# Ordering one program by PSUM bank: finer dependencies, and PSUM slots kept back by fences instead of by rule

## The chip, the cores and the metric

The kernel runs on one core of a Trainium2 chip. A core has five engines with queues of their own: TensorE (PE, matmuls; its weight loads are shown as PEld), VectorE (DVE), ScalarE (ACT), GpSimd (POOL) and SyncE (SP, which here issues the DMAs). PE writes its results to PSUM, 128 partitions of eight banks of 512 fp32 numbers; ACT and DVE read them there. The metric is the device time of one execution in microseconds, as the median of several runs; lower is better.

## What is computed

One inference step of a hybrid diffusion backbone of two layers, for 512 latent tokens and 128 context tokens that share all weights. The widths are D = 1024 and 2816 in the feed-forward part, all in fp32. Cut to what matters:

```python
def trunk_layer(x, cvec, l, P, pos, ctx):
    mod = jax.nn.silu(cvec) @ P['ada_w'][l] + P['ada_b'][l]
    sh1, sc1, g1, sh2, sc2, g2 = jnp.split(mod, 6, axis=-1)
    mix, ctx_out = token_mixer(x * (1.0 + sc1) + sh1, l, P, pos, ctx)
    x = layer_norm(ALPHA * x + g1 * mix, P['ln_g'][l, 0], P['ln_b'][l, 0])
    ff = conv_ffn(x * (1.0 + sc2) + sh2, l, P)
    x = layer_norm(ALPHA * x + g2 * ff, P['ln_g'][l, 1], P['ln_b'][l, 1])
    return x, ctx_out
```

token_mixer projects its input to three parallel mixers: A is retention in both directions with a fixed decay per head, B is gated linear attention in both directions with a decay that depends on the data, C is differential attention (two softmax maps per head). Each gives 512 channels, goes through a branch matrix, is weighted by sigmoid gates (also projections) and summed; an output projection follows. conv_ffn projects up to 2 x 2816, applies a depthwise convolution of width 3 and GELU to one half, multiplies the halves and projects down. The outputs are both token groups, and the context's keys, values and final states.

## The kernel before

All 640 tokens are handled together, channels on the 128 partitions and tokens along the free axis (512 latent, then 128 context). An activation of 1024 channels is eight tiles of 128 x 640. A fp32 product is made of three fast matmuls: each operand is split into a high part (hi, hh, ...) and a rest (lo, hl, ...), and hi*hi, hi*lo and lo*hi are added up in PSUM. Weights come block by block (128 x 1024) from HBM through three staging slots (w), are split by ACT (whi) and by DVE or POOL (wlo), and a block waits for a free slot of whi and wlo.

**How the order is found.** The functions of the kernel (mix_b, mix_a, mix_c, branch, the norms, the feed-forward part) don't emit instructions. Each call of mm, act, tt, ts and so on adds an operation to a Program (Program.add): the engines that may run it, an assumed cost, and the tiles and regions that it reads and writes. Program.add derives from these which earlier operations it depends on. When all are recorded, Program.order (L261) plays the whole program through on a model of the engines, greedily: whenever an engine is free it takes, among the operations whose inputs are ready and for which all new tiles can be given a slot, the one that was recorded first (with small exceptions, such as ACT's function tables). An operation may start before earlier ones as long as it lies within 120 us of PE work of the first unfinished matmul (40 us for loads). Program.issue then emits the instructions in the order of their modelled starts, so each engine's queue on the chip is in that order; waits are put in for true dependencies. The model's times do not reach the chip, only the order does.

**Slots.** Tiles live in pools (Pool_): `r`, 59 rows of 128 x 640 in SBUF, the weights' three pools, two small ones, and two PSUM pools of two slots each, a slot being 128 x 1024, two banks. `pp` (called through slot) takes most projections, the values pvv, the branch products and the mixers' accumulators po; `pm` (called through mslot) takes mixer B's pk, the decays pz, the scores psd, psl and psp of its levels, the states pst, mixer A's and C's scores, the norms' statistics (pm, pv, pn, pca, ...), and every other tile of the output, up and down projections (pfb, odd pout and pdn). A slot is given when the first operation on a tile is placed, and comes free when the last is done.

`reserve` is a rule of a pool: while no more than that many slots are free, only the tiles that come next in program order may take one (slots, within order). The rows have 7, `pp` has RES[0] = 0 and `pm` has RES[1] = 1, so with two slots the last free one of `pm` goes to the next tile in program order only.

**Dependencies.** For a tile in SBUF, Program.add compares regions (partitions and columns). For a PSUM tile it takes every access for an access of the whole tile (L238).

**Tiles and names around the change.** A projection (project, gemm) fills columns 256 to 896 of its slot in two halves, HALF: first tokens 256 to 640 in columns 512 to 896 (384 columns, second bank), then tokens 0 to 256 in columns 256 to 512 (first bank), for each half k = 0 to 7 and three matmuls per k. Its evictions mostly read both halves; rope has one that reads the context part alone (columns 768 to 896). v_proj fills blocks of tokens, in mixer B's first pass one bank for each token block. At the start the inputs hh/hl are made k by k, both halves of a k (to_h); at the layers' border and ahead of the feed-forward part they come from norm_h, one half after the other. mix_b makes two passes (t = 0, 1) over two heads each: decays (zr with pz), scores of the same position (psd), seven levels m = 1 to 64 (psl and copies into st; psp for the context), then m = 128 and 256, and at the end po, which all chunks add to. All is ordered as described; no line sets an order by hand.

Of the kernel before, what the change touches and what calls it, by code (L numbers as in the profile page):

```python
# [131 lines left out]
DEPTH = 2  # L132
SAME = 130
GAP = 2
RES = (0, 1)


class Tile_:
# [79 lines left out]
class Program:  # L218
# [3 lines left out]
    def add(self, engs, fn, outs, ins, cost, func=None, load=False, late=0, port=()):  # L222
        op = Op()
        op.idx, op.engs, op.fn, op.cost = len(self.ops), engs, fn, cost
        op.users, op.ready, op.func, op.load, op.eng = [], 0.0, func, load, None
        op.queues, op.port = set(), port
        op.key = (op.idx + late, op.idx)
        op.coord = self.pe
        if engs[0] == "PE":
            self.pe += cost["PE"]  # L230
        deps, tiles = set(), []
        for views, write in ((ins, False), (outs, True)):
            for v in views:
                if not isinstance(v, V):
                    continue
                t, (p0, p1, c0, c1) = v.tile, v.reg
                if t.pool is not None and t.pool.psum:
                    p0, p1, c0, c1 = 0, 128, 0, 1  # L238
                if t not in tiles:
                    tiles.append(t)  # L240
                keep = []
                for a in t.acc:
                    o, w, (q0, q1, d0, d1) = a
                    hit = p0 < q1 and q0 < p1 and c0 < d1 and d0 < c1
                    if hit and (w or write) and o is not op:
                        deps.add(o)
                    if not (write and p0 <= q0 and q1 <= p1 and c0 <= d0 and d1 <= c1 and o is not op):
                        keep.append(a)
                t.acc = keep
                t.acc.append((op, write, (p0, p1, c0, c1)))  # L250
        for t in tiles:
            if not t.left and t.pool is not None:
                t.pool.want.append((op.idx, t))
            t.left += 1
        op.deps, op.tiles, op.wait = sorted(deps, key=lambda o: o.idx), tiles, len(deps)
        for d in op.deps:
            d.users.append(op)
        self.ops.append(op)
        return op

    def order(self, ahead, ahead_load):  # L261
        import heapq
        engs = ("PE", "ACT", "DVE", "POOL", "SP")
        free = {e: 0.0 for e in engs}
        now, later = {e: [] for e in engs}, {e: [] for e in engs}
        held, done = [], []
# [16 lines left out]
        def slots(op, t0):  # L283

            used = {}
            for t in op.tiles:
                if t.slot is None and t.pool is not None:
                    p = t.pool
                    u = used.get(p, 0)
                    used[p] = u + 1  # L290
                    if len(p.free) <= u:
                        p.blocked.append(op)
                        return None
                    if p.inorder or len(p.free) <= p.reserve:
                        while p.want[p.ptr][1].slot is not None:
                            p.ptr += 1
                        i, rank = p.ptr, 0
                        lim = 1 if p.inorder else len(p.free)
                        while rank < lim and p.want[i][1] is not t:
                            rank += p.want[i][1].slot is None  # L300
                            i += 1
                        if rank >= lim:
                            p.blocked.append(op)
                            return None
                    t0 = max(t0, heapq.nsmallest(u + 1, p.free)[u][0])
            return t0
# [4 lines left out]
        while len(done) < len(self.ops):  # L311
            best = None
            for e in engs:
                f, n, q = free[e], now[e], later[e]
                while q and (q[0][0] <= f or q[0][2].eng):
                    r, i, op = heapq.heappop(q)
# [3 lines left out]
                while n or q:  # L320
                    if n:
                        i, op = heapq.heappop(n)
                        if op.eng:
                            continue
                        t = slots(op, f)
                        if t is not None and e in op.port:
                            t = max(t, port)
                        if t is None:
                            op.queues.discard(e)
                            continue  # L330
                        if t > f:
                            heapq.heappush(q, (t, i, op))
                            continue
                        if e == "POOL" and len(op.engs) > 1 and max(free["DVE"], op.ready) + op.cost["DVE"] <= t + op.cost[e]:
                            waiting.append((i, op))
                            continue
                        if e == "ACT" and op.func in TABLES and not table & TABLES[op.func] and passed < 6 and len(skipped) < 6 \
                                and op.key[0] >= op.idx:
                            skipped.append((i, op))
                            continue  # L340
                        cand = (t, i, op)
                        break
                    if skipped:
                        break
                    r, i, op = heapq.heappop(q)
                    if op.eng:
                        continue
                    t = slots(op, r)
                    if t is not None and e in op.port:
                        t = max(t, port)  # L350
# [8 lines left out]
                if cand is None and skipped:  # L359
                    i, op = skipped.pop(0)  # L360
# [8 lines left out]
                    else:  # L369
                        heapq.heappush(later[e], cand)  # L370
            if best is None:
                raise RuntimeError(f"stuck after {len(done)} of {len(self.ops)} operations: " + "; ".join(
                    f"{p.name}: {len(p.free)} free" for p in {o.tiles[0].pool for o in self.ops} if p))
            (t0, i, op), e = best
            c = op.cost[e]
            if e == "ACT" and op.func in TABLES:
# [38 lines left out]
            if e == "PE":  # L415
# [3 lines left out]
                while held:  # L419
                    o = held[0][2]  # L420
# [34 lines left out]
def hybrid_kernel(ctx, tc, io):  # L455
# [8 lines left out]
    def pool(name, n, space=sb, **kw):  # L464
        def make(t):
            return space.tile(t.shape, t.dt, tag=f"{name}{t.slot}", name=t.name)

        return Pool_(name, n, make, psum=space is psum, **kw)
# [3 lines left out]
    p_small, p_tiny = pool("sm", 2), pool("ti", 24)  # L472
    p_p, p_m = pool("pp", 2, psum, reserve=RES[0]), pool("pm", 2, psum, reserve=RES[1])

# [1173 lines left out]
```

## Time and profile before

| | us |
|---|---|
| median of 3 runs | 2575.58 (2574.66 to 2575.99) |
| the profiled execution | 2572.64 |
| its span, first to last instruction | 2570.9 |
| TensorE's mean granted clock | 0.981 of full speed |

The span in 40 slices, each digit the busy share in tenths; PEclk is the granted clock in tenths:

```profile
PE   7999999999998999999989899999999999999997
DVE  6688786576688765656868877644553574334446
ACT  3586754454225322213447766544442352132224
PEclk9999999999998999999989989999999999999998
```

A row of these profiles names a line, an engine, an operation, out<-in by the tiles' names, shapes and a count. Since every matmul is recorded by one helper (L504, L513 for pairs of 64 rows, L518 for transposes), the tile's name tells the stage. "[4.73 <-DVE qq]" behind a row says that the engine stood idle for 4.73 us before it, and what released it. Matmuls are pipelined: one lasts longer than the distance to the next, so the rate is read from the starts. The first layer takes about the first half: mixers to 730 us, output projection and norm to 838, feed-forward part to some 1290; the second layer repeats it.

### The profile page before, as it was taken

The numbers are of one execution on the slowest core, as the hardware profiler recorded it, in microseconds if no ns is written. First come the engines' busy times: TensorE is split into PE (matmuls) and PEld (weight loads), VectorE is DVE, ScalarE is ACT, GpSimd is POOL, SyncE is SP. The second block draws the span as 40 slices with busy tenths as digits, with TensorE's granted clock in tenths as the row PEclk, the third lists the DMA queues.
The fourth block names the chain that finished last, engine by engine and source line by source line (L and its number), as shares of the span: only waits on it lengthen the run. The fifth ranks groups of instructions, "written<-read, shape, count | busy, mean of one in ns | idle before, by whom it ended". The sixth has DMA issues, their size and how long they took to land.

```text
span 2570.9 us, 41226 instructions
## 1 busy us (share of the span) xinstructions
PE 2469.6 (96%) x16730; PEld 2349.8 (91%) x16730; DVE 1633.3 (64%) x2897; ACT 1126.3 (44%) x1822; POOL 515.1 (20%) x381
## 2 busy tenths in 40 slices
PE   7999999999998999999989899999999999999997
PEld 4888889999997999999978788999999989999996
DVE  6688786576688765656868877644553574334446
ACT  3586754454225322213447766544442352132224
POOL 0542120121334100101446501111111140000000
PEclk9999999999998999999989989999999999999998
DMA  7122222322442333333521221212113322222223
GB/s 278 49 93 85 89 72 93 104 88 99 156 156 99 123 108 120 108 116 130 163 98 53 68 89 60 62 52 75 52 66 115 112 77 82 75 74 74 74 76 105
DMA packets 92062, 248.76 MB, mean 97 GB/s; under 512 B 10336, under 2 KB 16864, under 8 KB 91744
## 3 DMA queue, kind: packets, MB, share of 16 engines
q1 hardware_dynamic: 91872, 246.13, 28.9%
q8 instruction: 131, 2.15, 0.3%
q14 instruction: 59, 0.48, 0.1%
HBM read 238.75 MB, written 7.34 MB: 96 GB/s over the span
## 4 chain that ended last, share of the span: by engine, by line
PE 85%; DVE 8%; ACT 4%; DMA 1%; issue 1%; POOL 1%; SPq 0%; ACTq 0%; DVEq 0%; POOLq 0%
PE pmm L504 13%; PE pfb L504 12%; PE pfa L504 11%; PE pdn L504 11%; PE pbr L504 7%; PE pvv L504 6%; PE pout L504 4%; PE pck L504 2%; PE pcq L504 2%; PE pag L504 2%; PE psc L513 2%; PE ptc L504 1%; PE psl L513 1%; PE po L504 1%; DVE hl L551 1%
## 5 line engine op out<-in xcount | busy, mean ns | idle before, releaser
L525 ACT ACTIVATE whi<-w 128x1024 fp32r<-128x1024 f32 (+2 forms) x330 | 342.9, 1040 | 864.0 <-PE pdn L504 221.5
L537 DVE TENSOR_TENSOR wlo<-w,whi 128x1024 fp32r<-128x1024 f32 (+2 forms) x276 | 344.0, 1247 | 356.9 <-ACT whi L525 350.7
L537 POOL TENSOR_TENSOR wlo<-w,whi 128x1024 fp32r<-128x1024 f32 (+1 forms) x54 | 130.2, 2412 | 806.6 <-ACT whi L525 664.7
L504 PE MATMUL pmm<-hl,whi 128*128 128x384 f32 (+1 forms) x768 | 239.3, 312 | 0.0
L504 PE MATMUL pmm<-hh,whi 128*128 128x384 f32 (+1 forms) x768 | 238.9, 311 | 0.0
L504 PE MATMUL pmm<-hh,wlo 128*128 128x384 f32 (+1 forms) x768 | 238.8, 311 | 0.0
L504 PE MATMUL pfa<-hl,whi 128*128 128x384 f32 (+1 forms) x704 | 221.4, 315 | 7.2 <-DVE hl L551 6.8
L504 PE MATMUL pfa<-hh,whi 128*128 128x384 f32 (+1 forms) x704 | 219.5, 313 | 5.4 <-ACT hh L525 5.3
L504 PE MATMUL pfb<-hh,wlo 128*128 128x256 f32 (+1 forms) x704 | 220.1, 313 | 3.9 <-DVE wlo L537 3.9
L504 PE MATMUL pdn<-fh,whi 128*128 128x384 f32 (+1 forms) x704 | 217.6, 310 | 2.7 <-DVE xa L551 2.7
L504 PE MATMUL pfb<-hh,whi 128*128 128x256 f32 (+1 forms) x704 | 220.1, 313 | 0.0
L504 PE MATMUL pfb<-hl,whi 128*128 128x256 f32 (+1 forms) x704 | 219.9, 312 | 0.0
L504 PE MATMUL pfa<-hh,wlo 128*128 128x384 f32 (+1 forms) x704 | 219.5, 312 | 0.0
L504 PE MATMUL pdn<-fh,wlo 128*128 128x384 f32 (+1 forms) x704 | 218.0, 310 | 0.0
L504 PE MATMUL pdn<-fl,whi 128*128 128x384 f32 (+1 forms) x704 | 217.5, 309 | 0.0
L504 PEld LDWEIGHTS pmm<-hh,whi 128*128 128x128 f32 x768 | 144.5, 188 | 1.2 <-issue 1.1
L504 PEld LDWEIGHTS pmm<-hh,wlo 128*128 128x128 f32 x768 | 144.5, 188 | 0.9 <-issue 0.6
L504 PEld LDWEIGHTS pmm<-hl,whi 128*128 128x128 f32 x768 | 144.4, 188 | 0.9 <-issue 0.5
L504 PEld LDWEIGHTS pfa<-hl,whi 128*128 128x128 f32 x704 | 133.8, 190 | 10.5 <-DVE hl L551 10.4
L504 PE MATMUL pvv<-whi,hh 128*128 128x256 f32 (+1 forms) x480 | 138.1, 288 | 4.9 <-ACT hh L525 3.9
L504 PEld LDWEIGHTS pfa<-hh,whi 128*128 128x128 f32 x704 | 133.5, 190 | 7.4 <-ACT hh L525 7.3
L504 PE MATMUL pvv<-wlo,hh 128*128 128x256 f32 (+1 forms) x480 | 137.5, 287 | 2.7 <-DVE wlo L537 2.7
(388 smaller groups left out, 6829.2 us busy)
## 6 DMA issues: line engine op xcount, KB each, us to landing
w<-W SPq DMA_DIRECT2D x276, 512.0 KB, 3.5
wada<-adaT SPq DMA_DIRECT2D x160, 256.0 KB, 3.9
w<-W SPq DMA_DIRECT2D x48, 448.0 KB, 3.2
wada<-adaW SPq DMA_DIRECT2D x32, 256.0 KB, 5.2
x<-xT SPq DMA_DIRECT2D x8, 320.0 KB, 6.1
dist<-rc SPq DMA_DIRECT2D x8, 320.0 KB, 3.4
xa<-xT SPq DMA_DIRECT2D x8, 320.0 KB, 6.7
xsave<-xa SPq DMA_DIRECT2D x8, 320.0 KB, 6.1
```

The lines of the kernel that those rows point to most:

```text
L504: prog.add(("PE",), lambda e: nc.tensor.matmul(real(out), real(lhsT), real(rhs), start=start, stop=stop), [out], [lhsT, rhs], {"PE": c})
L513: nc.tensor.matmul(real(o), real(w), real(r), start=start, stop=stop)
L525: prog.add(("ACT",), lambda e: nc.scalar.activation(out=real(out), in_=real(in_), func=func, **{k: real(x) for k, x in kw.items()}), [out] ...
L537: prog.add(eng, lambda e: ENG[e].tensor_tensor(out=real(out), in0=real(a), in1=real(b), op=op), [out], [a, b], vcost(out.n), late=late, po ...
L551: prog.add(eng, lambda e: ENG[e].scalar_tensor_tensor(out=real(out), in0=real(a), scalar=real(s), in1=real(b), op0=op0, op1=op1), [out], [ ...
```

## The change

Three things change; no operation is added to or taken from the program that is ordered.

- In Program.add the region of an access to a PSUM tile becomes the range of 512-column banks that it touches, on all partitions, instead of the whole tile.
- RES becomes (0, 0): no slot of `pm` is kept back by rule.
- Without a reserve the order can get stuck (all slots held by tiles whose last operations need another slot). order becomes a loop around the former function, now place. If place ends with operations left over, the loop takes the first operation that has no engine, waits for no input and needs a new slot, and adds a fence for the pools concerned: as long as that operation is not placed, all operations behind it in program order must leave one slot of the pool free (two at most). Then all is reset and placed again, up to 60 times.

```diff
-RES = (0, 1)
+RES = (0, 0)
...
                 if t.pool is not None and t.pool.psum:
-                    p0, p1, c0, c1 = 0, 128, 0, 1
+                    p0, p1, c0, c1 = 0, 128, c0 // 512, -(-min(c1, 1024) // 512)
...
     def order(self, ahead, ahead_load):
+
+
+        fences, tiles = {}, {t: t.left for o in self.ops for t in o.tiles}
+        pools = {t.pool: list(t.pool.free) for t in tiles if t.pool is not None}
+        for _ in range(60):
+            done = self.place(ahead, ahead_load, fences)
+            if len(done) == len(self.ops):
+                return done
+            for f in self.ops:
+                new = [p for p in {t.pool for t in f.tiles if t.slot is None and t.pool is not None}]
+                if not f.eng and not f.wait and new and any(fences.get((p, f), 0) < 2 for p in new):
+                    break
+            else:
+                break
+            for p in new:
+                fences[p, f] = fences.get((p, f), 0) + 1
+            for o in self.ops:
+                o.eng, o.ready, o.wait, o.queues = None, 0.0, len(o.deps), set()
+            for t, n in tiles.items():
+                t.slot, t.left, t.end = None, n, 0.0
+            for p, free in pools.items():
+                p.free, p.blocked, p.ptr = list(free), [], 0
+        raise RuntimeError(f"stuck after {len(done)} of {len(self.ops)} operations")
+
+    def place(self, ahead, ahead_load, fences):
...
-                    if len(p.free) <= u:
+                    if len(p.free) <= u + sum(n for (q, f), n in fences.items() if q is p and not f.eng and op.idx > f.idx):
                         p.blocked.append(op)
                         return None
...
             if best is None:
-                raise RuntimeError(f"stuck after {len(done)} of {len(self.ops)} operations: " + "; ".join(
-                    f"{p.name}: {len(p.free)} free" for p in {o.tiles[0].pool for o in self.ops} if p))
+                break
```

## The prediction

> **What bounds the kernel now.** I read the page first: the busy line, then the chain that ended last.
>
> ```profile
> span 2570.9 us, 41226 instructions
> PE 2469.6 (96%) x16730; PEld 2349.8 (91%) x16730; DVE 1633.3 (64%) x2897; ACT 1126.3 (44%) x1822; POOL 515.1 (20%) x381
> PE 85%; DVE 8%; ACT 4%; DMA 1%; issue 1%; POOL 1%; SPq 0%; ACTq 0%; DVEq 0%; POOLq 0%
> ```
>
> TensorE (PE) is busy for 2469.6 of 2570.9 us, and 85% of the chain is PE work. The change reorders instructions and removes none, so all that it can win or lose is PE's idle time, 2570.9 - 2469.6 = 101.3 us, and time in which PE runs at a lower granted clock. Where these lie is told by busy time in 65 us stretches. Columns: stretch, its length, busy us (and instructions) of PE, its weight loads, DVE, ACT, POOL; granted clock; DMA share; GB/s.
>
> ```profile
> 0.00:65.00 65.00, 49.81 (x248) 28.18 (x249) 39.60 (x154) 25.34 (x53) 4.21 (x10) 0.95 0.74 278
> 130.00:195.00 65.00, 59.50 (x457) 53.20 (x456) 52.75 (x75) 51.18 (x100) 26.63 (x26) 1.00 0.27 92
> 195.00:260.00 65.00, 58.67 (x401) 52.63 (x401) 54.58 (x87) 44.45 (x87) 19.04 (x17) 0.92 0.28 92
> 780.00:845.00 65.00, 52.31 (x287) 47.95 (x286) 56.22 (x112) 34.24 (x58) 35.10 (x28) 0.84 0.25 81
> 1365.00:1430.00 65.00, 59.92 (x488) 53.21 (x486) 50.88 (x62) 43.32 (x85) 41.39 (x39) 0.97 0.17 56
> 1430.00:1495.00 65.00, 51.91 (x393) 45.74 (x392) 56.47 (x86) 47.58 (x94) 32.94 (x31) 0.87 0.20 65
> 2015.00:2080.00 65.00, 62.20 (x396) 60.55 (x394) 47.19 (x94) 29.69 (x44) 14.09 (x8) 0.95 0.38 122
> 2145.00:2210.00 65.00, 65.00 (x443) 65.00 (x442) 27.91 (x40) 18.10 (x21) 0.00 (x0) 1.00 0.23 73
> ```
>
> The reader should see a stretch without any idle time (2145, the feed-forward part: nothing to win) beside the start (15.2 us idle), the two passes of mixer B (130 to 260 and 1365 to 1495) and the step from the output projection to the feed-forward part (780). Now who PE waited for; columns: total us, times, longest.
>
> ```profile
> PE pq L504 <- ACT hh L525: 7.5, 5, 3.5
> PE pfa L504 <- DVE hl L551: 6.8, 6, 2.5
> PE pm L504 <- DVE acc L537: 5.2, 2, 4.1
> PE psl L513 <- DVE qq L580: 4.7, 1, 4.7
> PE po L504 <- ACT qa L525: 3.1, 1, 3.1
> PE psl L513 <- DVE st L572: 2.6, 2, 1.3
> ```
>
> The first four are waits for data, the last two for a PSUM slot still being read. Slots alone are a small part of the idle time.
>
> **Part 1: dependencies by bank (Program.add).** It removes the order between accesses of one PSUM tile that lie in different 512-column banks. Where does that free PE? A projection fills columns 512 to 896 first (the 384-column half) and then 256 to 512: by whole tiles the second half may not begin before the first is complete, by banks it may. At the start of the kernel the inputs hh/hl arrive one k at a time:
>
> ```profile
> 45.72 0.45 PE L504 MATMUL pq<-hh,whi 128*128 128x384 f32 x1 [0.60 <-ACT hh L525]
> 47.77 0.44 PE L504 MATMUL pq<-hh,whi 128*128 128x384 f32 x1 [0.58 <-ACT hh L525]
> 49.90 0.45 PE L504 MATMUL pq<-hh,whi 128*128 128x384 f32 x1 [0.53 <-ACT hh L525]
> 50.84 0.28 PE L504 MATMUL pq<-hh,whi 128*128 128x256 f32 x1
> 53.67 0.34 PE L504 MATMUL pk<-hl,whi 128*128 128x384 f32 x1
> 54.02 0.28 PE L504 MATMUL pk<-hh,whi 128*128 128x256 f32 x1
> 56.86 0.30 PE L504 MATMUL pvv<-whi,hh 128*128 128x288 f32 x1
> 57.00 0.29 PE L504 MATMUL pvv<-whi,hl 128*128 128x288 f32 x1
> ```
>
> A k arrives each 2.1 us; from 45.72 to 49.90 PE runs for each k the three wide matmuls of pq and of pk and then waits. All narrow ones come after the last wide one: pq's 24 from 50.84 to 53.67 (118 ns each), pk's 24 from 54.02 to 56.86 (118 ns each). By banks those of k = 0 to 6, 2 x 7 x 3 = 42 with 42 x 0.118 = 5.0 us, can run in the gaps: to_h writes both halves of a k before the next k. Wide ones cost 0.175 us (pk's two from 53.67 to 54.02), so six are 1.05 us of each 2.1 us, and six narrow ones 0.7 us: they fit. I take 4.5 us of the 5.0, since a mixture of two tiles never packs wholly. What hides the rest today is nothing: after 50.84 PE is busy without a gap, so the saving moves all that follows. Late next would be the weights of pvv, whose slots pq and pk free earlier by the same amount. Bounds: 0 (weights late) and 6.3 (with the nine matmuls of pvv's second token block, which lie in its other bank: 9 x 0.14 us from 56.86 to 57.00).
>
> At the border of the layers PE waits in the same way:
>
> ```profile
> 1310.33 0.29 PE L504 MATMUL pvv<-wlo,hh 128*128 128x288 f32 x1
> 1312.97 0.39 PE L504 MATMUL pq<-hh,whi 128*128 128x256 f32 x1 [2.35 <-ACT hh L525]
> ```
>
> But there half 0 of every k is made before half 1 (norm_h goes half by half), so the halves are not each other's filler. Only pvv's nine of the second token block can fill such a wait: 1 us. In the other tiles the evictions read both banks (P0:P0+T), so they stay where they are; rope's 128-column copy of the context part reads the first-filled bank alone and may go some 3 us (24 narrow matmuls) earlier, but it waits for its turn on ACT rather than for PE, so I count 0, from -1 to +3. No instruction or DMA is added, and SP's loads move only with the matmuls that free their slots.
>
> **Part 2: no slot of pool pm kept back (RES 1 to 0), with fences.** Before, the last free of the two pm slots went only to the next tile in program order. Here is what that shapes in mixer B of the second layer:
>
> ```profile
> 1347.41 0.45 PE L504 MATMUL pz<-zr,wa 128*128 128x384 f32 x2
> 1349.67 0.56 PE L504 MATMUL pz<-zr,wa 128*128 128x384 f32 x2 [0.52 <-DVE la L545]
> 1375.50 1.16 PE L513 MATMUL psl<-eq,ek 64*128 64x128 f32 x16 [1.30 <-DVE st L572]
> 1388.80 0.53 PE L504 MATMUL pz<-zr,wa 128*128 128x384 f32 x2
> 1452.01 0.28 PE L504 MATMUL paq<-hh,wlo 128*128 128x256 f32 x1
> 1477.68 0.77 PE L513 MATMUL psl<-qq,kk 128*128 128x256 f32 x2 [4.73 <-DVE qq L580]
> 1482.02 0.80 PE L513 MATMUL psl<-qq,kk 128*128 128x256 f32 x2 [1.18 <-ACT p L525]
> 1487.28 0.27 ACT L525 ACTIVATE qa<-paq 128x128 f32<-128x128 f32 x1
> 1487.61 1.65 PE L504 MATMUL po<-st,v 128*128 128x128 f32 x6 [3.05 <-ACT qa L525]
> ```
>
> The decay matmuls pz of t = 0 run at 1347 and 1349. Those of t = 1 read the same zr and wa, so they could run then, but start at 1388.80, 39 us later, when both slots are free at once. From them hangs t = 1's chain of levels, at whose end PE stands still: 4.73 + 1.18 us, then 3.05 us for a slot of the other pool, pp, which the change does not touch. Earlier decays let that chain end earlier. The value is not shown by any row, so it has two ends. The best end is all that two passes lose: in 130 to 260, 5.50 + 6.33 us idle and 0.08 x 65 = 5.2 us of clock; in 1365 to 1495, 5.08 + 13.09 us idle and (0.03 + 0.13) x 65 = 10.4 us: 45.6 us. The worst end is a loss of 18 us (rival 2). I take 6 us, the two waits of the chain's end in this row set (5.9), and nothing for the first layer, because DVE there is already busy for 52.75 and 54.58 of 65 us.
>
> The clock column bears on this: 0.87 in 1430 to 1495 costs 8.5 us beside the idle time itself. [...]
>
> **Sum.** 4.5 + 1 + 6 = 11.5 us: the span goes from 2570.9 to 2559.4. The profiled execution took 2572.64 us, 1.74 more than its span, and the median of the runs, 2575.58, lies 2.94 above that. So 2575.6 - 11.5 = 2564 us as a median.
>
> **Rivals.**
> 1. **The gain is swallowed (2573).** For it: 780 to 845 and the ends of the layers wait for data (hh, hl, acc), and a new greedy order may lose there what it wins elsewhere; the step at 780 has 12.7 us of idle time where the same step of the second layer (2015 to 2080) has 2.8, so an order alone can move 10 us. Against: the start's 4.5 us have no wait behind them that stays. About 2 to 3 us remain.
> 2. **Hoarded slots (2588, slower).** A tile far ahead takes the last pm slot and its readers do not get their turn; then t's chain has one slot, and each level waits until the level before has been read out. Price: the 1.30 us at 1375.50, where pk held the other slot. Seven levels, two t, two layers are 28; the half that has little other PE work beside it, 14 x 1.30 = 18 us; less 5.5 for part 1 it is +12.5. It decides once more than four levels are hit uncovered (4 x 1.30 = 5.2 against part 1's 5.5). For it: paq's last matmul starts at 1452.01, and its slot is held until 1487.28, so slots are held for 35 us in this kernel. Against: a fence keeps a slot back, though only where the order got stuck altogether.
> 3. **The starvation goes (2546).** t = 1's chain overlaps t = 0's wholly, in both layers: of the 45.6 us some 24 come back, with part 1's 5.5 together 29.5. Against: DVE's 52 to 56 busy us of 65 leave it little room.
> 4. **It does not do what it says** (waits on the chip remain by tile): PE would then wait for each early reader of the first bank. That is inside rival 1 up to three waits of the size of 1.30 us, and beyond that it is like rival 2.
>
> **How the numbers follow.** Forecast 2564, its own range 2557 to 2570: 0.43. Rival 1: 0.20. Rival 2, with 4's worse half: 0.25. Rival 3: 0.12. A difference under 0.2%, about 5 us, is no more than a measurement can tell from no change. Faster 0.43 + 0.12 = 0.55, same 0.20, slower 0.25. The range reaches from rival 3's middle to nearly rival 2's price: 2546 to 2586, which leaves out about half of rival 3 and something less than half of rival 2.
>
> **What would show it.** Part 1: narrow pq and pk matmuls between the wide ones before 50 us, and the first pvv after them about 5 us before 56.86. Part 2: the second pair of pz well before 1388.80 (less the shift), and a PE idle time under 10 us where 1430 to 1495 has 13.1. Rival 2: more and longer waits psl <- st than the 2.6 us above, in mixer B. The feed-forward stretches should stay at 65.00 of 65. It is wrong if idle time grows in a stretch that I count as unchanged, above all 780 to 845 and the two ends of layers.

## The result, and the profile after

The changed kernel takes 2558.41 us as a median (2556.14 to 2559.82) against 2575.5 beside it: ratio 0.9933, 95% interval 0.9916 to 0.9950, 17 us faster. The page and its busy line:

```profile
span 2554.4 us, 41254 instructions
PE 2462.3 (96%) x16730; PEld 2344.1 (92%) x16730; DVE 1635.9 (64%) x2895; ACT 1128.1 (44%) x1822; POOL 520.0 (20%) x385
```

As many matmuls as before, so the work is the same; of the 16.5 us of span 9.2 were idle time (2554.4 - 2462.3 = 92.1 against 101.3) and the rest is busy time (2462.3 against 2469.6), at a mean granted clock of 0.986 against 0.981. The same stretches as in the prediction, now of the changed kernel:

```profile
0.00:65.00 65.00, 49.84 (x246) 29.11 (x247) 37.48 (x150) 25.13 (x53) 4.27 (x10) 0.96 0.73 274
130.00:195.00 65.00, 63.14 (x499) 56.61 (x497) 55.04 (x70) 50.05 (x97) 37.64 (x36) 1.00 0.28 92
195.00:260.00 65.00, 60.76 (x410) 54.10 (x410) 55.84 (x96) 47.44 (x90) 12.89 (x10) 0.95 0.30 98
780.00:845.00 65.00, 52.70 (x306) 49.48 (x306) 59.02 (x112) 35.55 (x59) 35.99 (x28) 0.89 0.28 94
1365.00:1430.00 65.00, 63.68 (x511) 57.19 (x512) 52.48 (x64) 50.56 (x93) 37.20 (x39) 1.00 0.24 80
1430.00:1495.00 65.00, 53.83 (x414) 47.47 (x413) 57.17 (x103) 46.34 (x94) 24.65 (x25) 0.89 0.21 68
2145.00:2210.00 65.00, 65.00 (x444) 65.00 (x443) 25.59 (x39) 15.49 (x17) 0.00 (x0) 1.00 0.24 79
```

The start does as much as before (49.84 busy us, 246 instructions), mixer B of both layers does more, the feed-forward part is full as it was. And the waits of PE:

```profile
PE po L528 <- DVE qa L561: 8.7, 1, 8.7
PE pfa L528 <- DVE hl L575: 7.4, 6, 2.6
PE pck L528 <- ACT qkp L549: 2.9, 8, 0.4
PE pcq L528 <- ACT qkp L549: 2.9, 8, 0.4
PE psl L537 <- DVE st L596: 1.5, 2, 1.3
PE pvv L528 <- ACT z L549: 1.5, 4, 0.4
```

Three rows are of a new kind: pck and pcq waiting for ACT's qkp, and pvv for z. They are short and regular, and those for qkp come from rope's early copies, which the prediction had counted as 0. The first row has grown: po waited 3.05 us for qa before.

Since the operations are the same and only their order differs (and for some the engine that runs them), I compare where the kernels stand at fixed points of the program. The first line has the times before; below it is each kernel's lead or lag there (minus: earlier), read from the timeline as the start of the first matmul of that tile in that layer (for pdn and pq a fixed one of them).

```
                      start      B1       A,C1     step    border   B2      A2      C2     span
                      psl   paq   pag   pcq  pout  pdn    pq     pag   pcq   pout
before                97.4 169.1 240.6 347.4 731.8 1108.7 1313.0 1514.3 1622.7 2007.1  2570.9
changed               -0.6  +0.3  -5.4  -8.4  -2.3  -5.8   -7.1  -16.2  -20.8  -15.4   2554.4
e1_banks_only         -4.2  +0.7  +2.5  +4.7  +9.8  +5.0   +4.0   -1.1   -1.3   +3.1   2572.9
e2_slots_only         +0.7  +0.8  +1.6  -0.1  +0.1  -2.9   -3.1  -12.4  -14.3  -14.4   2557.2
e3_readers_whole      -0.4  -2.5  -7.7 -11.1  -9.6 -13.2  -16.1  -26.5  -31.2  -30.8   2538.6
e4_rope_whole         +0.8  +1.7  -4.0  -7.5  -6.7 -10.9  -13.6  -21.3  -26.0  -25.2   2545.1
e6_start_wide_first   -2.3  -4.2  -9.2 -12.6 -11.1 -15.0  -17.7  -29.3  -34.0  -33.5   2535.7
e7_start_after_ada    -4.0  -6.0 -11.7 -15.0 -13.4 -16.5  -16.2  -28.4  -33.1  -32.6   2537.8
e8_late_decays        -2.8  -2.7  +3.9  +2.4  +2.3  -2.0   -3.6   -9.9  -13.2  -12.1   2558.0
e10_rope_by_bank      -2.9  -4.9  -9.9 -12.9  -7.0 -10.4  -12.0  -23.2  -27.7  -22.2   2547.6
```

Each row is one execution, so small leads mean little. In the changed kernel and e4_rope_whole PE's rows name the same tiles in the same order to far beyond the first paq (for 2261 matmuls), and yet the two stand 1.4 us apart there; whole executions of the kernel before lie between 2570.67 and 2578.40 us.

The line "changed" tells the story. Nothing is won at the start (paq +0.3). Mixer B of the first layer wins some 6 us; mixer C and the branches give 6 back between pcq and pout (some of pcq's lead is work moved ahead, from then on 3 to 4 us are lost); the step to the feed-forward part wins 3.5; mixer B of the second layer wins 9; its mixer C gives back 5 by the same count. The step's 3.5 belong to neither part alone: every other kernel in the table wins 3.0 to 4.8 there, the banks alone and the slots alone too. Whether the kernel before loses them in each execution is not shown.

### The profile page after: what moved, and what is told of

It reads as the page before. It is cut to its first block, busy times and chain, and to the rows that moved or that the text cites. A ratio compares the mean times of both kernels' runs of the same rounds, so it can differ in the third digit from the quotient of the medians.

```text
span 2554.4 us, 41254 instructions
## 1 busy us (share of the span) xinstructions
PE 2462.3 (96%) x16730; PEld 2344.1 (92%) x16730; DVE 1635.9 (64%) x2895; ACT 1128.1 (44%) x1822; POOL 520.0 (20%) x385
## 5 line engine op out<-in xcount | busy, mean ns | idle before, releaser
L561 DVE TENSOR_TENSOR wlo<-w,whi 128x1024 fp32r<-128x1024 f32 (+1 forms) x278 | 345.0, 1242 | 363.5 <-ACT whi L549 356.8
L528 PE MATMUL pfb<-hl,whi 128*128 128x384 f32 (+1 forms) x704 | 219.6, 312 | 0.0
L528 PE MATMUL pfb<-hh,whi 128*128 128x384 f32 (+1 forms) x704 | 218.8, 311 | 0.0
```

Source lines behind the costliest of these rows:

```text
L528: prog.add(("PE",), lambda e: nc.tensor.matmul(real(out), real(lhsT), real(rhs), start=start, stop=stop), [out], [lhsT, rhs], {"PE": c})
L561: prog.add(eng, lambda e: ENG[e].tensor_tensor(out=real(out), in0=real(a), in1=real(b), op=op), [out], [a, b], vcost(out.n), late=late, po ...
```

## The experiments

### The two parts alone

```diff
 e1_banks_only
-RES = (0, 0)
+RES = (0, 1)
 e2_slots_only
-                    p0, p1, c0, c1 = 0, 128, c0 // 512, -(-min(c1, 1024) // 512)
+                    p0, p1, c0, c1 = 0, 128, 0, 1
```

> Only the dependencies by bank; pool pm keeps its last slot for the next tile in program order again. Theory (mixer B's gain of some 17 us in its two layers comes from the freed slots, and the banks bring about nothing at the start and a loss of some 3 us in each mixer C, where ACT's early copies qkp stand between the matmuls of one projection): 2575 to 2582 us, no gain in mixer B, and 16 waits of PE for ACT qkp of about 0.37 us. Rival (the banks make the gain): 2556 to 2564 us, with the earlier mixer B of the changed kernel.

> Only the freed slots with fences; PSUM dependencies by whole tile as before. Theory: mixer B's gain without the losses of the banks, 2550 to 2556 us, no waits of PE for ACT qkp, and t = 1's decays pz some 10 us or more earlier in each layer than before. Rival (the slots alone do nothing, or hoarding makes it slower): 2572 us or more.

The banks alone gave 2574.87 us, ratio 1.0002 (0.9992 to 1.0011): no change. The slots alone gave 2559.33, ratio 0.9934 (0.9917 to 0.9950): as much as the whole change. The slots bring the gain, though 3 us less than the theory's range; the banks bring nothing on balance. The table shows that the second is a balance and not a zero: with the banks alone the kernel loses 5 us from pcq to pout in the first layer and 4 in the second, and wins 5 at the step and, against the theory, 5 in mixer B of the second layer. The slots' gain lies in the second layer (pq to pag, 9 us) and at the step, not in the first layer's mixer B, where the slots alone do nothing (pag +1.6). There the 5.4 us of the changed kernel need both parts.

In the second layer the slots alone do what the prediction said of them: the waits of 4.73, 1.18 and 3.05 us at the end of t = 1's chain are gone, and the idle time from 1430 to 1495 falls from 13.09 to 6.05 us. The row of e2_slots_only:

```profile
1430.00:1495.00 65.00, 58.95 (x439) 52.52 (x437) 53.89 (x82) 41.79 (x87) 31.96 (x30) 0.89 0.16 52
```

But early decays alone don't explain it. In the first layer the decays of t = 1 start at 119.82 us instead of 142.29 in e2, 22 us earlier, and mixer B wins nothing; in the second they start at 1380.59 instead of 1388.80, only 5 us closer to t = 0's, and it wins 9.

### What the banks cost

One of the new waits, on PE's timeline of the changed kernel, and then the row of ACT that belongs to it:

```profile
454.79 0.34 PE L528 MATMUL pcq<-hh,wlo 128*128 128x384 f32 x1
454.96 0.28 PE L528 MATMUL pcq<-hh,whi 128*128 128x256 f32 x1
...
456.38 0.28 PE L528 MATMUL pcq<-hh,whi 128*128 128x256 f32 x1
456.50 0.27 PE L528 MATMUL pcq<-hl,whi 128*128 128x256 f32 x1
457.15 0.38 PE L528 MATMUL pcq<-hh,wlo 128*128 128x256 f32 x1 [0.37 <-ACT qkp L549]
```

```profile
456.82 0.28 ACT L549 ACTIVATE qkp<-pcq 128x128 f32<-128x128 f32 x1 [2.77 <-PE pcq L528]
```

ACT's copy qkp reads columns 768 to 896, the bank that the wide half had filled before the narrow matmuls (256 columns) began. The last wide one has ended at 455.13. Yet ACT, idle for 2.77 us, starts only at 456.82, just after the 14th narrow one has ended (456.50 + 0.27 = 456.77), and the 15th then waits for ACT; the other nine follow later, from 458.93. So the waits in the program treat the tile as one here: the reader waits for the matmuls that stand before it in the order, whatever their bank, and those that stand behind it wait for the reader. All 18 early copies of this run (16 qkp, 2 ka) start 0.03 to 0.05 us after the end of the matmul before them, and PE's next one starts 0.05 or 0.06 us after the copy's end. An order that takes the two banks for independent puts the reader between the matmuls, and PE pays. PE's step from 456.50 to 457.15 is 0.65 us instead of 0.12: 0.53 us for one copy. The 18 such steps of the changed kernel (16 for qkp, 2 for ka) are 0.64 to 0.73 us long.

```diff
 e3_readers_whole
-                    p0, p1, c0, c1 = 0, 128, c0 // 512, -(-min(c1, 1024) // 512)
+                    p0, p1, c0, c1 = (0, 128, c0 // 512, -(-min(c1, 1024) // 512)) if engs[0] == "PE" else (0, 128, 0, 2)
 e4_rope_whole
-        act(prompt, ps[:, P0 + TL:P0 + T])
+        act(prompt, ps[:, P0 + TL:P0 + T], also=(ps,))
```

(`also` adds its tiles to what the operation reads for the order; the instruction is the same.)

> As the changed kernel, but by banks only between accesses of TensorE; ACT's and DVE's accesses to a PSUM tile count for the whole tile. Theory (the chip's waits go by whole tile, so each reader that the order puts between the matmuls of its tile costs PE about 0.37 us, some 23 of them, 8 to 9 us): 2548 to 2553 us, and no waits of PE for qkp, ka or z. Rival (these waits cost nothing in the end, or another order loses as much elsewhere): 2556 to 2565 us.

> As the changed kernel, but rope's copy of the context part (qkp, qa, ka) counts for the whole tile. Theory: 16 + 2 waits of 0.37 us go, 6.7 us, so 2550 to 2554 us, and mixer C no longer gives back 3 us in each layer. Rival (the 3 us in each mixer C come from something else): mixer C gives back 3 us as before, 2556 to 2561 us.

e3_readers_whole gave 2542.83 us, ratio 0.9876 (0.9862 to 0.9891), and e4_rope_whole 2546.86, 0.9892 (0.9875 to 0.9908). Both are faster than the changed kernel by more than expected: 0.0057 x 2575 = 14.7 us and 10.6 us, each good to some 5 us by the intervals. In both, qkp no longer holds PE up, and mixer C gives nearly nothing back (pcq to pout 1.5 and 0.8 us where it was 6.1). In size both theories were short, because I had counted PE's idle time alone, 0.37 us where the step loses 0.53. The idle time of the weight loads is nearer to the loss:

```profile
PEld pcq L528 <- ACT qkp L549: 4.6, 8, 0.6
PEld pck L528 <- ACT qkp L549: 4.6, 8, 0.6
PEld pvv L528 <- ACT z L549: 2.4, 4, 0.6
PEld pak L528 <- ACT ka L549: 1.1, 2, 0.6
```

These four rows of the changed kernel add up to 12.7 us, beside the 14.7 of e3; qkp and ka alone are 10.3, near the 10.6 of e4. Against the slots alone, e3_readers_whole (banks between matmuls only) is faster by 0.0058, some 15 us: that is what the banks bring once no reader stands between the matmuls, and what the readers take back in the changed kernel. By the table 6 of the 15 arise in the first layer's mixer B (paq to pag); why is not shown. On the fastest base found (e6, below) I put the cost back by itself:

```diff
 e10_rope_by_bank (against e6_start_wide_first)
-                    p0, p1, c0, c1 = (0, 128, c0 // 512, -(-min(c1, 1024) // 512)) if engs[0] == "PE" else (0, 128, 0, 2)
+                    p0, p1, c0, c1 = (0, 128, c0 // 512, -(-min(c1, 1024) // 512)) if engs[0] == "PE" or self.bank else (0, 128, 0, 2)
...
+        prog.bank = True
         act(prompt, ps[:, P0 + TL:P0 + T])
+        prog.bank = False
```

> As e6_start_wide_first, but rope's copy of the context part alone counts by bank again. Theory (each such copy cuts a projection in two for PE; the idle time of PE is 0.37 us each, that of its weight loads 0.57 us): 16 waits for qkp and 2 for ka are back, PE idle 6.7 us, the time 7 to 11 us longer: 2545 to 2549 us, and each mixer C gives back 3 to 5 us. Rival (the copies cost nothing, the gain of e4_rope_whole was another order): 2536 to 2541 us.

It gave 2550.45 us, ratio 0.9907 (0.9892 to 0.9921) against e6's 0.9865: 10.8 us slower by the ratios, at the upper end of the expected 7 to 11 (the time itself lies above the expected 2549). The waits are back, as in the changed kernel:

```profile
PE pck L528 <- ACT qkp L549: 2.9, 8, 0.4
PEld pcq L528 <- ACT qkp L549: 4.6, 8, 0.6
PEld pck L528 <- ACT qkp L549: 4.6, 8, 0.6
```

18 copies for 10.8 us are 0.6 us each, against 0.53 in the row shown. By the table most of the difference arises in the two mixers C (from pcq to pout 5.9 and 5.5 us are lost, where e6 loses 1.5 and 0.5), and about 1 us at the border of the layers.

### Why the start gains nothing

The changed kernel does run the narrow matmuls early. But before the last inputs there are matmuls with more to say, pada, whose results scale the inputs k = 4 to 7. Its last transposes before the change:

```profile
39.74 0.66 PE L518 MATMUL pada<-cst,ev 128*128 128x128 f32 x4 [0.69 <-ACT ev L525]
```

And now:

```profile
39.45 0.28 PE L528 MATMUL pq<-hh,wlo 128*128 128x256 f32 x1
39.66 1.04 PE L528 MATMUL pada<-wada,sc 128*32 128x512 f32 x2
...
42.45 0.39 PE L528 MATMUL pk<-hl,whi 128*128 128x256 f32 x1
42.68 0.28 PE L528 MATMUL pk<-hh,wlo 128*128 128x256 f32 x1
43.21 0.66 PE L542 MATMUL pada<-cst,ev 128*128 128x128 f32 x4 [0.25 <-ACT ev L549]
...
56.12 0.40 PE L528 MATMUL pvv<-whi,hh 128*128 128x288 f32 x1 [0.97 <-ACT q L549]
...
61.65 0.40 PE L528 MATMUL pvv<-wlo,hh 128*128 128x288 f32 x1 [1.96 <-DVE wlo L561]
```

The narrow matmuls stand between the pada ones, pada ends 3.5 us later, and so the inputs come later (ACT's first hh after pada starts at 46.28 instead of 42.81). Then pvv waits 0.97 us for a slot and 1.96 for weights whose slot pq frees only at its end, now 54.7 where it was 53.8. Two kernels, each on the base of e3:

```diff
 e6_start_wide_first and e7_start_after_ada
-                mm(o, wh[:, a], xh[:, c0:c1], start=(k == 0), stop=False)
+                mm(o, wh[:, a], xh[:, c0:c1], start=(k == 0), stop=False, also=late if c0 == 0 else ())
...
+    first = [1, 1]
 e6: the narrow half of the first pq and pk after the wide one
+        gemm(ps, w, 0, 8, hs, late=(ps,) if first and first.pop() else ())
 e7: after the last result of pada
+        gemm(ps, w, 0, 8, hs, late=(mods[0],) if first and first.pop() else ())
```

> As e3_readers_whole, but in the first two projections of the program (pq, pk) the narrow half waits for the wide half again. Theory (the narrow matmuls run early put off the pada matmuls, by 4.9 us in e3_readers_whole, and so the inputs, and this eats what they win): pada ends as in the kernel before, within 1 us, the first paq comes within 2 us of e3_readers_whole's, and the time is the same within 3 us, 2540 to 2546 us. Rival (the start's filling is worth its 4.5 us): the first paq comes 4 us later, 2546 to 2549 us.

> As e3_readers_whole, but the narrow half of the first two projections waits until the last pada is evaluated. Theory: pada ends as in the kernel before, the narrow matmuls fill only the gaps from 43 to 51 us, and the start is 2 to 3 us earlier than in e6_start_wide_first: 2538 to 2542 us. Rival (the weights of pvv, whose slots come free when pq and pk end, or the wait for z set the start in any case): within 1 us of e6_start_wide_first at the first psl.

e6 gave 2537.98 us, ratio 0.9865 (0.9848 to 0.9881), e7 2537.9, 0.9861 (0.9846 to 0.9875). In e6 pada's matmuls end 1.0 us later than before the change instead of 4.9, and paq comes 1.7 us earlier than in e3 (2.4 in e10, which starts as e6 does): filled in this way the narrow halves win nothing. Filled behind pada (e7), they seem to win a further 1.8 us at paq (1.1 against e10), a little less than expected and hardly more than two executions of one order differ by. That lead is gone at the layers' border (-16.2 against -17.7). In the whole time e3, e6 and e7 cannot be told apart.

### The decays, and the slots of the other pools

```diff
 e8_late_decays (against e6)
+        st0 = []
         def decays(t):
...
-                       start=True, stop=True)
+                       start=True, stop=True, also=st0)
...
+            st0 = st
             qd = []
 e5_last_pp_slot (against e3)
-RES = (0, 0)
+RES = (1, 0)
 e9_rows_free (against e6)
-    p_row = pool("r", NR, reserve=7)
+    p_row = pool("r", NR)
```

> As e6_start_wide_first (2538.0 us), but the decay matmuls pz of t = 1 wait until the levels 1 to 64 of t = 0 are done. Theory of the prediction (the freed slots gain in mixer B because t = 1's decays go out early): mixer B of the second layer loses its 11 us again, and perhaps some of the first layer's: 2549 us or more. Rival (the freed slots gain by letting any ready tile of pm fill PE, the decays being only one of them, and t = 1's chain starts when its q and k are there in any case): 2536 to 2542 us.

It gave 2561.77 us, ratio 0.9950 (0.9935 to 0.9965), 22 us slower than e6. The decays of t = 1 start at 1397.96 there, 58 us behind those of t = 0, where the kernel before has 41 (1388.80 - 1347.41) and the changed kernel 37, by its timeline:

```profile
1337.25 0.75 PE L528 MATMUL pz<-zr,wa 128*128 128x384 f32 x4
1374.13 0.46 PE L528 MATMUL pz<-zr,wa 128*128 128x384 f32 x2
```

In e8 PE waits for the levels' operands instead; its waits between 1300 and 1520 us begin with

```profile
PE psl L537 <- DVE eq L561: 14.4, 4, 6.9
```

So holding the decays back costs time in mixer B: in the first layer the lead at pag turns from -9.2 to +3.9, in the second the stretch from pq to pag wins 6.3 instead of 11.6 us. But the 22 us are not the share that the freed slots owe to early decays. In the second layer e8 holds them back further than the old rule did; in the first it holds them less far (54 us behind those of t = 0, where the kernel before has 63), and its mixer B is still 6.6 us slower than before. In the second layer the changed kernel's pz are only 4 us closer to those of t = 0. With e2's first layer, where early decays won nothing, this leaves open how the freed slots make their 9 us: by the decays, or by letting any ready tile of pm fill PE.

> As e3_readers_whole, but the other PSUM pool, pp, keeps its last slot for the next tile in program order. Theory (paq and pak take both pp slots far ahead of their readers, and mixer B's po waits 8.7 us for DVE's qa in the second layer; a kept slot lets po begin when its own inputs are there): this wait goes, and 5 to 9 us of 2542.8 with it, 2534 to 2538 us. Rival (a kept slot in the pool of the projections takes away work done ahead, and PE stands idle elsewhere): 2543 us or more.

2574.22 us, ratio 1.0001 (0.9992 to 1.0011): the rival, and far beyond it. The 8.7 us wait of po does go, but a slot of pp kept back costs 31 us against e3, and now other waits lead:

```profile
PE psl L537 <- DVE st L596: 9.3, 4, 3.7
```

> As e6_start_wide_first, but the SBUF rows keep back none of their 59 either (reserve 7 to 0; fences where the order gets stuck). Theory (the 8.7 us wait of po for DVE's qa stands for want of a row that the rule keeps back): this wait falls under 3 us and the time to 2529 to 2534 us. Rival (rows taken far ahead are missed by the chain, or DVE's own order sets that wait): 2536 us or more.

2540.41 us, ratio 0.9864 (0.9848 to 0.9880), no different from e6. The po wait of 8.7 us is gone from the list, as the theory had it, but it is gone in e2 and e5 too, so that the rows kept back cause it is not shown; and the time is not shorter: the first layer has lost 3 us by pout (8.0 us ahead of the kernel before, where e6 is 11.1 ahead).

## Why the prediction was right, and which steps were not

The forecast was 11.5 us, and 17 came; the direction and the likeliest case held. Its terms held less well than their sum, and that the sum came out near is in part luck: part 2 alone brings 17 us (e2) where 6 were counted; in part 1 some 15 us won between the matmuls, where 5.5 were counted, cancel against 14.7 lost by the readers, where none were.

**What bounds it**: right. Only PE's idle time and clock moved, and the feed-forward stretches stayed at 65.00 of 65.

**Part 1 at the start, 4.5 us: wrong, it was 0.** "After 50.84 PE is busy without a gap, so the saving moves all that follows" overlooked what stands ahead of 50.84: the gaps into which the narrow matmuls went were shared with pada, and pada sets when the inputs come. The first pvv behind the narrow matmuls starts at 56.12, not some 5 us before 56.86 as forecast. Done in this way the filling wins nothing (e6 against e3); behind pada it may bring 1 to 2 us.

**Part 1 at the border, 1 us**: 1.3 us came (pdn -5.8, pq -7.1); the banks alone win 1.0 there, the slots alone 0.2.

**Rope's early copy, "0, from -1 to +3": wrong, and the largest miss.** It costs 10.6 us in the changed kernel, and all readers by bank 14.7. I had seen that ACT could go earlier and taken it that PE would not notice. Rival 4 named the mechanism (waits on the chip remain by tile), but I put it at "up to three waits of the size of 1.30 us" without counting the copies: 18 of rope's, at 0.53 us.

**Part 2, 6 us in the second layer and nothing in the first: right in place, too small, and in the changed kernel not by the waits priced.** The wait of 4.73 us and that of 1.18 that I priced are gone; but the third, po's, which I left out as one of pool pp, grew from 3.05:

```profile
1467.74 2.08 PE L528 MATMUL po<-st,v 128*128 128x128 f32 x8 [8.66 <-DVE qa L561]
```

Together the three were 8.96 us, so in the changed kernel the chain's end gave only 0.3, and the idle time from 1430 to 1495 is 11.17 us, not under 10 as forecast; the slots alone do bring it to 6.05. More came from 1365 to 1430, where idle time fell from 5.08 to 1.32 us and the clock rose from 0.97 to 1.00. In the first layer 5.4 us came where I had none, on the argument that DVE was busy: DVE is a little busier still (55.04 and 55.84), but PE found other work meanwhile (499 and 410 matmuls against 457 and 401). The slots alone do not give that.

**The step at 780**, which I listed as a place that might turn the forecast over, won 3.5 us, by my estimate mostly by the clock: idle time there is 12.3 us against 12.7, the granted clock 0.89 against 0.84 (0.05 x 65 = 3.3 us). The idle time is nearly equal, but it lies elsewhere: from 795 to 805 PE was idle for 2.1 us at a granted clock of 0.52 before, and is not idle now, at 0.76. What lowers the clock there is not shown by any run.

**Rival 2, hoarded slots**: not seen with pm; waits of psl for st fell from 2.6 to 1.5 us. **Rival 1** held at one place: what was won in mixer B was partly swallowed in mixer C.

The best versions run are e6 and e7, both at about 2538 us: with the freed slots, dependencies by bank between matmuls alone, and the start's narrow halves behind the wide ones or behind pada.

## What to carry to other kernels

A finer dependency in the program that finds the order helped here only as far as the waits in the instructions are as fine (some 15 us won between matmuls, 14.7 lost again to the readers put between them): ask of each pair of engines separately, and keep to the coarser rule where an engine would be put between another's matmuls. Don't add up the parts of such a change: each part gives a new order, and here two parts that were worth nothing and 17 us alone were worth 32 once one kind of dependency was left coarse. When an order fills gaps with early work, look at what else lived in those gaps and what hangs on it. A pool's reserve was here a lever of tens of microseconds in either direction (pm freed: 17 faster; pp kept: 31 slower), so try each pool by itself.

## What was not expected of the hardware

A wait of PE in the midst of a projection cost more than its idle time: in the changed kernel 0.37 us of idle time between two matmuls made a step of 0.65 us instead of 0.12. The idle time is counted from the end of the matmul before (456.77), which in the narrow half otherwise overlaps the next one by some 0.16 us (0.28 long, 0.12 apart), and 0.37 + 0.16 is the 0.53 lost. The weight load of the next matmul, which otherwise runs beside the one before it (456.39 to 456.58, beside the matmul of 456.38 to 456.66), waited too (PEld idle 0.57 us there).
